# Layer kernel with a state-space scan on one Trainium2 core: both directions' scans in one instruction stream, more of the small work on VectorE, and a reordered step in the attention

## The chip, the cores and the metric

The kernel runs on one core of a Trainium2 chip. The core has TensorE (PE: matrix products, whose weights are loaded by a separate stream, PEld), VectorE (DVE), ScalarE (ACT), GpSimd (POOL) and SyncE (SP, which here only starts transfers). Each engine works through its own queue in order, and semaphores connect them. Transfers between DRAM and the on-chip memory go through queues that an engine's own instructions feed. The metric is device time of one execution in microseconds (us). TensorE's clock has two levels, 1.2 and 2.4 GHz, and the profile shows the granted one as a fraction of full speed.

## What is computed

Two layers act on 1024 latent and 256 context tokens of width 1024. In each layer a normalised, modulated input goes through one wide projection, whose output columns are shared among four mixers: an attention with 4 heads (A), a pooling mixer (B), a two-way complex state space (C) and a spatial gating (D). Their gated outputs go through one output projection and a normalisation. The change touches A, B and above all C:

```python
def _s5_scan(u, disc, reverse, h0):                       # 16 groups of 64 complex states
    lb_re, lb_im, bb_re, bb_im = disc
    bu_re = jnp.einsum('bngh,gph->nbgp', u, bb_re)        # and bu_im
    ...
    _, _, hr, hi = lax.associative_scan(_cscan_combine, (a_re, a_im, bu_re, bu_im),
                                        reverse=reverse, axis=0)   # h[t] = lb * h[t-1] + bu[t]

def _s5_readout(hr, hi, c_re, c_im):
    return jnp.einsum('nbgp,ghp->bngh', hr, c_re) - jnp.einsum('nbgp,ghp->bngh', hi, c_im)

def _pool_mixer(vin, w_pool, scale):                      # windows 2, 4, 8, 16
    ...                                                   # centred means minus the input
    y = jnp.einsum('bngc,gcd->bngd', pooled.reshape(b, n, N_POOL, POOL_GC), w_pool)
    return y.reshape(b, n, BRANCH_W) * scale

    # attention, for 128 queries at a time
    s = einsum('bqhd,bkhd->bhqk', qn, k_nope) + einsum('bqhr,bkr->bhqk', qr, k_rope)
    p = jax.nn.softmax(s * scale, axis=-1)
    return jnp.einsum('bhqk,bkhd->bqhd', p, vf)
```

In the second layer only the latent tokens' output is needed.

## The kernel before

All engines' instructions are written in program order in one file, and a scheduler places each engine's queue from it by that order as priority, except where the kernel fixes the order by hand (the attention, the first section and the output projection). Generators with `yield` are the unit in which `layer` (L1723 to L1928) interleaves the mixers' small work with the projection's weight blocks. A weight block is loaded (`wraw`), rounded on ScalarE into a high half (`whi`, L638), and VectorE takes the low half (`wlo`, helper line L131) as the difference. TensorE multiplies the high and low halves with the input's halves (L152 to L154), so a block's last third waits for VectorE. A generic helper at L131, L144 or L148 issues nearly all two-operand operations, so rows carry that line, and the tiles' names tell them apart.

The state space works on blocks of 8 tokens, 160 block positions ("slots": 128 latent, 32 context) in all.

- `s5_operators` (L505 to L634) makes a layer's operators. `outer` (L563 to L577) is six instructions on 128x512 elements: four products and two combinations. VectorE calls it for the input operators (tiles `op2`, `op3` and scratch `op0`). GpSimd calls it for the readout operators (tile `R`, one for all four calls, with the scratch `op1`), and GpSimd's queue then stores `R` to DRAM in two transfers (`Rd`). TensorE transposes the input operators (`tp_s5op`, L598), ScalarE copies and stores them (`Ed`). A short kernel of lags follows (`Kd`).
- `s5_states` (L733 to L758) loads the blocks' inputs, and TensorE makes what each slot adds to the state. ScalarE copies each PSUM tile to `H`, a tile [128, direction, 8, re/im, 161] with the slots in order along the last axis (L755 to L758). `H` lies on memory that the operators' pool (`ops`) has held.
- `s5_scan` (L760 to L854) cuts the 160 slots into 5 segments of 32 and advances all five at once, one slot per step, 31 steps. Each step and direction has a product of 160 elements (8 rows, two parts, two operands, 5 segments at a stride of 32) and two additions of 80, with the two directions interleaved. Ahead of it a table of powers (`pws`) is made, one direction on VectorE, the other on GpSimd. Behind it the segments are joined: for each of the four borders and each direction five small instructions carry the state, and five instructions on 496 or 248 elements fix up the segment. VectorE does five of these eight blocks, GpSimd three (`PFIX`). At the end four transfers on GpSimd's queue exchange the halves of `H` through DRAM (`Xd`, L850 to L853).
- `s5_readout` (L856 to L898) builds the short kernel's weights (`M`, ScalarE, L868) and makes the output on TensorE: for 16 operators each, one product with the inputs (L888), one with the backward states (L891), and with the forward states one (128 columns, L892) and in layer 0 another (32, L894). The moving operand is a contiguous stretch of `H`.
- `pool_mix` (L958 to L985) makes the windows' sums, on GpSimd for the first of its two blocks of channels (`b` 0) and on VectorE for the second.
- The attention's order is given by hand (L1480 to L1532): it passes over the queries, two heads at a time, and for each pass over pieces of the keys. In each pass, VectorE takes the rows' maxima (`maxima`), then at the mark `m4` the low parts of the next queries (`QA`, `QB`: two subtractions), then writes the maximum rows (`rows`, L144) that TensorE needs for the shift (L1376) and the sums (L1435).

## Time and profile before

| | us |
|---|---|
| median of 3 runs | 1434.23 (1432.74 to 1434.94) |
| profiled execution | 1430.7, span 1428.9 |
| TensorE busy, share of the span | 1252.1, 88% |
| VectorE busy | 932.5, 65% |
| GpSimd busy | 554.7, 39% |
| ScalarE busy | 467.6, 33% |
| mean granted clock of TensorE | 0.95 |

Busy times are of the profiled execution. Register, branch and transfer-starting instructions do not count as busy. In the timelines a line begins with its start and the time that the group on it spans, and ends with the idle time before it in brackets and what ended that, where that counts. `out<-in` are the tiles' names, `xN` how many instructions the line stands for.

### The profile page before, as it was taken

How to read it: one execution, taken by the hardware profiler on the slowest of the kernel's cores; microseconds unless marked ns; L12 is line 12 of the kernel's file. 1: busy time of each engine (PE TensorE's matmuls, PEld its weight loads, DVE VectorE, ACT ScalarE, POOL GpSimd, SP SyncE). 2: the span in 40 equal slices, each digit the busy share in tenths (PEclk: the TensorE clock that was granted, in tenths of full speed). 3: DMA queues.
4: the chain of work that ended last, by engine and by line, in shares of the span. 5: the costliest groups of instructions: out<-in, count | busy, mean ns of one | idle time of the engine just before them, and what ended most of it. 6: DMA issues, size and time to landing. Idle time of an engine off the chain costs nothing.

```text
span 1428.9 us, 19998 instructions
## 1 busy us (share of the span) xinstructions
PE 1252.1 (88%) x7556; PEld 962.6 (67%) x7556; DVE 932.5 (65%) x1812; ACT 467.6 (33%) x879; POOL 554.7 (39%) x580
## 2 busy tenths in 40 slices
PE   3877994999999998999999869987599998998997
PEld 1555773779878766666777647765488786665685
DVE  7685399642543566767798882599517456767666
ACT  2341130121244644445243322301213454544300
POOL 2467230500102254665444592224101136756443
PEclk9887997999999989999999979998889999999999
DMA  9435322476320100014123444412662020000421
GB/s 322 135 94 177 115 85 75 117 199 151 83 57 19 45 23 1 1 42 133 48 74 103 100 140 158 138 45 59 135 161 66 11 60 23 30 2 16 150 101 73
DMA packets 124677, 127.31 MB, mean 89 GB/s; under 512 B 40908, under 2 KB 98724, under 8 KB 124582
## 3 DMA queue, kind: packets, MB, share of 16 engines
q1 hardware_dynamic: 118886, 111.86, 26.8%
q0 software_dynamic: 2880, 9.54, 2.8%
q10 hardware_dynamic: 2816, 4.65, 0.9%
q8 instruction: 59, 0.97, 0.3%
q14 instruction: 36, 0.29, 0.1%
HBM read 97.47 MB, written 25.94 MB: 86 GB/s over the span
## 4 chain that ended last, share of the span: by engine, by line
PE 51%; DVE 29%; POOL 6%; issue 6%; DMA 4%; ACT 3%; SPq 1%; DVEq 0%; POOLq 0%; ACTq 0%
PE mm_out L1637 7%; PE mm_sc L1332 6%; PE mm_in L154 6%; PE mm_in L152 6%; PE mm_in L153 6%; DVE H L131 5%; DVE stmp L131 3%; DVE z L148 3%; DVE acc L131 2%; PE av L1415 2%; DVE op L131 2%; PE mm_sc L1374 1%; POOL op L131 1%; DMA M<-Kd 1%; DVE xres L145 1%
## 5 line engine op out<-in xcount | busy, mean ns | idle before, releaser
L154 PE MATMUL mm_in<-hT,wlo 128*128 128x512 f32 (+1 forms) x696 | 264.9, 381 | 26.0 <-DVE wlo L131 26.0
L153 PE MATMUL mm_in<-hT,whi 128*128 128x512 f32 (+1 forms) x696 | 265.1, 381 | 5.0 <-POOL hT L131 2.5
L152 PE MATMUL mm_in<-hT,whi 128*128 128x512 f32 (+1 forms) x696 | 269.0, 388 | 0.4 <-ACT whi L638 0.4
L154 PEld LDWEIGHTS mm_in<-hT,wlo 128*128 128x128 f32 x696 | 136.8, 197 | 53.6 <-DVE wlo L131 28.7
L1637 PE MATMUL mm_out<-wo,yh 128*128 128x512 f32 x576 | 164.2, 398 | 1.8 <-DVE wo L131 1.7
L152 PEld LDWEIGHTS mm_in<-hT,whi 128*128 128x128 f32 x696 | 136.6, 197 | 36.9 <-issue 14.2
L153 PEld LDWEIGHTS mm_in<-hT,whi 128*128 128x128 f32 x696 | 136.5, 196 | 31.4 <-POOL hT L131 5.3
L1637 PEld LDWEIGHTS mm_out<-wo,yh 128*128 128x128 f32 x576 | 107.3, 188 | 29.9 <-DVE wo L131 3.3
L638 ACT CAST whi<-wraw 128x1024 fp32r<-128x1024 f32 x38 | 42.6, 1121 | 194.6 <-PE mm_in L153 146.8
L131 DVE TENSOR_TENSOR wlo<-wraw,whi 128x1024 fp32r<-128x1024 f32 x38 | 58.0, 1530 | 68.0 <-ACT whi L638 61.7
L131 DVE TENSOR_TENSOR acc<-acc,mm_sc 128x512 f32<-128x512 f32 x108 | 74.2, 687 | 42.3 <-PE mm_sc L1332 31.2
L131 POOL TENSOR_TENSOR psum<-pE 128x512 f32<-128x512 f32 (+1 forms) x36 | 47.4, 1318 | 124.2 <-ACT pE L1393 124.1
L1637 PE MATMUL mm_out<-wo,yl 128*128 128x512 f32 x288 | 93.1, 395 | 0.3 <-POOL yl L131 0.3
L131 POOL TENSOR_TENSOR psum<-psum,pL 128x512 f32<-128x512 f32 x64 | 83.2, 1300 | 6.4 <-ACT pL L1393 1.5
L131 DVE TENSOR_TENSOR H<-H,stmp 128x80 f32<-128x80 f32 x248 | 74.6, 355 | 0.8
L144 POOL TENSOR_SCALAR rs_z<-mv_z 128x1 f32<-128x1 f32 x18 | 18.5, 1029 | 119.9 <-DVE mv_z L1669 119.9
L144 POOL TENSOR_SCALAR srs<-smv 128x1 f32<-128x1 f32 x18 | 5.6, 310 | 152.6 <-DVE smv L1065 152.6
L1637 PEld LDWEIGHTS mm_out<-wo,yl 128*128 128x128 f32 x288 | 54.2, 188 | 13.4 <-POOL yl L131 0.8
L131 DVE TENSOR_TENSOR stmp<-a,H 128x160 f32<-128x160 f32 x124 | 53.3, 462 | 14.6 <-POOL pws L131 7.2
L1393 ACT ACTIVATE pE<-mm_sc 128x512 f32<-128x512 f32 x55 | 30.7, 595 | 95.0 <-PE mm_sc L1374 73.7
L1621 ACT CAST yh<-G 128x1024 fp32r<-128x1024 f32 x18 | 18.9, 1052 | 115.1 <-PE mm_out L1637 113.8
L1788 ACT ACTIVATE G<-mm_in 128x512 f32<-128x512 f32 (+1 forms) x40 | 22.2, 555 | 104.1 <-PE mm_in L154 104.0
(361 smaller groups left out, 2789.8 us busy)
## 6 DMA issues: line engine op xcount, KB each, us to landing
wmod<-in_w_mod_dram SPq DMA_DIRECT2D x48, 512.0 KB, 4.3
wraw<-in_w_in_dram SPq DMA_DIRECT2D x36, 512.0 KB, 4.1
wor<-in_w_out_dram SPq DMA_DIRECT2D x16, 512.0 KB, 3.5
s5u<-Sd SPq DMA_DIRECT2D x8, 640.0 KB, 7.3
xd<-z SPq DMA_DIRECT2D x10, 512.0 KB, 2.7
xin<-in_x_dram SPq DMA_DIRECT2D x8, 512.0 KB, 7.6
Ed<-E ACTq DMA_DIRECT2D x16, 256.0 KB, 3.0
Rd<-bldR POOLq DMA_DIRECT2D x16, 256.0 KB, 3.9
```

What stands on the lines that cost most here:

```text
L131: return e.tensor_tensor(out=out, in0=a, in1=b, op=op)
L144: return e.tensor_scalar(out=out, in0=a, scalar1=s1, scalar2=None, op0=op0)
L148: return V.scalar_tensor_tensor(out=out, in0=a, scalar=s, in1=b, op0=op0, op1=op1)
L152: T.matmul(out, lhsT=ahi, rhs=bhi, start=start, stop=False)
L153: T.matmul(out, lhsT=ahi, rhs=blo, start=False, stop=False)
L154: T.matmul(out, lhsT=alo, rhs=bhi, start=False, stop=stop)
L638: copy(hi, raw)
L1332: T.matmul(out, lhsT=K[:, e, 128 * kt_:128 * kt_ + 128], rhs=Q[:, f], start=(x == 0 and y == 0), stop=False, skip_group_check=True)
L1393: S.activation(out=p, in_=ps, func=AF.Exp, scale=QSCALE)
L1415: T.matmul(st[v][64 * h:64 * h + 64, 0:n], lhsT=Vt[:, BANKS[i // 2][i % 2], 64 * head:64 * head + 64], rhs=st[v, h]["pt"][i // 2][:, n * ( ...
L1637: T.matmul(a[1][nh], lhsT=y[u][:, k, :], rhs=self.W[k][:, v, 512 * nh:512 * nh + 512], start=(k == 0 and u == 0 and v == 0), stop=(k == KC ...
L1788: S.activation(out=G[ci][:, b, :], in_=ps, func=AF.Silu)
```

## The change

Four things are done.

1. The operators of the readout go from GpSimd to VectorE (`outer(V, ...)`). They stand behind all state operators and lag kernels, share their scratch tile, and alternate between `R` and a new tile `R2`, which lies in the operators' pool. Their eight stores stay on GpSimd's queue.
2. `H` holds the slots with the segments innermost: the five segments' slots of one step lie side by side (165 positions instead of 161), and the backward direction is stored mirrored. ScalarE's copies into `H` write with a stride of 5 elements, and so the moving operands in `s5_readout` are read. A scan step is one product of 320 elements and two additions of 160 for both directions. The table is made on VectorE alone. The four carries come in a row for both directions, and the fix-ups are 16 instructions on 8 x 31 x 4 elements, all on VectorE.
3. `pool_mix` of the first block goes from GpSimd to VectorE.
4. In the attention the mark `m4` (the next queries' low parts) stands behind the maximum rows.

```diff
-NPOS = 161
+NPOS = 165
 SEG = 32
-PFIX = (1, 2, 3)
...
-        tv_, tp_, w0, w1, BC = (sp.tile([128, 1024], F32, name="op%d" % i) for i in range(5))
+        tv_, R2, w0, w1, BC = (sp.tile([128, 1024], F32, name="op%d" % i) for i in range(5))
...
-            first = mul(e, a, lr, vr)
-            if e is P:
-                tc.keep_in_program_order(first)
+            mul(e, a, lr, vr)
             mul(e, b, li, vi)
             tt(e, dre, a, b, ALU.subtract if sgn > 0 else ALU.add)
             mul(e, a, lr, vi)
...
-            Rv = R.rearrange("p (r c q) -> p r c q", r=2, c=4)
             for c in (slice(0, 4), slice(4, 8)):
                 k0, step = ((7, -1), (0, 1))[d]
                 outer(V, tv_, ld, k0, step, [Bb[:, ri, 8 * d:8 * d + 8, :] for ri in range(2)], c, [w[:, c] for w in W], 1)
-
-                k0, step = ((1, 1), (8, -1))[d]
-                outer(P, tp_, ld, k0, step, [CT[:, ri, 8 * d:8 * d + 8, :] for ri in range(2)], c,
-                      [Rv[:, ri] for ri in range(2)], -1)
-                for ri in range(2):
-                    P.dma_start(Rd[l][:, c, 2 * d + ri, :], Rv[:, ri])
                 yield
-            yield
...
         P.dma_start(Kd[l][112:128, :], dd)
+        for d in range(2):
+            for i, c in enumerate((slice(0, 4), slice(4, 8))):
+
+                k0, step = ((1, 1), (8, -1))[d]
+                Rv = (R, R2)[i].rearrange("p (r c q) -> p r c q", r=2, c=4)
+                outer(V, tv_, 2 * l + d, k0, step, [CT[:, ri, 8 * d:8 * d + 8, :] for ri in range(2)], c,
+                      [Rv[:, ri] for ri in range(2)], -1)
+                for ri in range(2):
+                    P.dma_start(Rd[l][:, c, 2 * d + ri, :], Rv[:, ri])
+                yield
         drop("ops")
...
+    NSEG = NSLOT // SEG
+
+    def spread(x, dims):
+
+        return bass.AP(tensor=x.tensor, offset=x.offset, ap=[list(x.ap[0])] + dims)
...
         Hs[0] = H
-        V.memset(H[:, 0, :, :, 0:1], 0.0)
-        V.memset(H[:, 1, :, :, NSLOT:NPOS], 0.0)
+        V.memset(H[:, :, :, :, 0:1], 0.0)
         for d in range(2):
             for ri in range(2):
                 E = wr("Eld")
...
                     pv = ps[:, 0:np_ * NSLOT].rearrange("p (j c) -> p j c", j=np_)
-                    hv = H[:, d, p0:p0 + np_, ri, :]
+
+                    pv = pv.rearrange("p j (a b) -> p j a b", b=SEG)
+                    h = [[2 * NPOS, np_]]
                     if d:
-                        S.copy(hv[:, :, 0:NSLOT], pv)
+                        S.copy(spread(H[:, d, p0, ri, NPOS - 1:NPOS], h + [[-1, NSEG], [-NSEG, SEG]]), pv)
                     else:
-                        S.copy(hv[:, :, 33:NPOS], pv[:, :, 0:128])
-                        S.copy(hv[:, :, 1:33], pv[:, :, 128:NSLOT])
+                        S.copy(spread(H[:, d, p0, ri, NSEG + 1:NSEG + 2], h + [[1, NSEG - 1], [NSEG, SEG]]), pv[:, :, 0:NSEG - 1])
+                        S.copy(spread(H[:, d, p0, ri, NSEG:NSEG + 1], h + [[NSEG, SEG]]), pv[:, :, NSEG - 1])
...
-
-        for d in range(2):
-            for c in range(2):
-                tc.keep_in_program_order(E[d].tensor_copy(T2[:, d, c, :, 0], a8[:, l, d, :, 0, c]))
+        T2 = tab.rearrange("p (c x i) -> p c x i", c=2, x=16)
+        a8l = a8[:, l].rearrange("p d r k o -> p (d r) k o")
...
+
+        def states_at(i, dims):
...
+        for c in range(2):
+            V.tensor_copy(T2[:, c, :, 0], a8l[:, :, 0, c])
...
         while n < SEG:
...
+            b = [T2[:, c, :, n - 1:n].to_broadcast([128, 16, n]) for c in range(2)]
+            x = [T2[:, c, :, 0:n] for c in range(2)]
+            o = [T2[:, c, :, n:2 * n] for c in range(2)]
...
+            mul(V, o[0], b[0], x[0])
+            mul(V, m1, b[1], x[1])
+            mul(V, o[1], b[0], x[1])
+            mul(V, m2, b[1], x[0])
+            sub(V, o[0], o[0], m1)
+            add(V, o[1], o[1], m2)
             n *= 2
...
-            o = 160 * (2 * d + i % 2)
-            return tmp[:, o:o + 32 * n].rearrange("p (r k o s) -> p r k o s", r=8, k=2, o=2)
-
         for i in range(1, SEG):
-            xs_ = []
-            for d in range(2):
-                st = (SEG, -SEG)[d]
-                h = H[:, d, 0, 0, position(d, i - 1):position(d, i - 1) + 1]
-                x = x_tile(i, d, nseg)
-                mul(V, x.rearrange("p r k o s -> p (r k) o s"),
-                    a8[:, l, d].rearrange("p r k o -> p (r k) o").unsqueeze(3).to_broadcast([128, 16, 2, nseg]),
-                    ap(h, [[NPOS, 16], [0, 2], [st, nseg]]))
-                xs_.append(x)
+            x = tmp[:, 320 * (i % 2):320 * (i % 2) + 64 * NSEG].rearrange("p (x k o s) -> p x k o s", x=16, k=2, o=2)
+            mul(V, x.rearrange("p x k o s -> p (x k) o s"),
+                a8l.rearrange("p x k o -> p (x k) o").unsqueeze(3).to_broadcast([128, 32, 2, NSEG]),
+                states_at(NSEG * i, [[NPOS, 32], [0, 2], [1, NSEG]]))
+            h = states_at(NSEG * i + NSEG, [[2 * NPOS, 16], [NPOS, 2], [1, NSEG]])
...
-                for d in range(2):
-                    h = H[:, d, 0, 0, position(d, i):position(d, i) + 1]
-                    h = ap(h, [[2 * NPOS, 8], [NPOS, 2], [(SEG, -SEG)[d], nseg]])
-                    add(V, h, h, xs_[d][:, :, k])
+                add(V, h, h, x[:, :, k])
             yield
...
+        xc = sml.tile([128, 64], F32, tag="xc", name="xc", bufs=1)
+        x1, x2 = (xc[:, 32 * i:32 * i + 32].rearrange("p (x o) -> p x o", x=16) for i in range(2))
+        re, im = (T2[:, c, :, SEG - 1:SEG].to_broadcast([128, 16, 2]) for c in range(2))
+        for k in range(1, NSEG):
+            h, hc = (states_at(NSEG * SEG + j, [[2 * NPOS, 16], [NPOS, 2]]) for j in (k - 1, k))
+            mul(V, x1, re, h)
+            mul(V, x2, im, h)
+            add(V, hc, hc, x1)
+            sub(V, hc[:, :, 0], hc[:, :, 0], x2[:, :, 1])
+            add(V, hc[:, :, 1], hc[:, :, 1], x2[:, :, 0])
+        V.tensor_copy(states_at(1, [[NPOS, 32], [1, NSEG - 1]]), states_at(NSEG * SEG, [[NPOS, 32], [1, NSEG - 1]]))
+        yield
...
-        mv_ = [s2("sm1")[:, 0:496], s2("sm2")[:, 0:496]]
-        mp_ = [tmp[:, 0:496], tmp[:, 496:992]]
...
-            for d in range(2):
-                e, (m1, m2) = (P, mp_) if (d == 1 and k in PFIX) else (V, mv_)
-                prev = position(d, SEG * k - 1)
-                re, im = (T2[:, d, c, :, 0:w].unsqueeze(2).to_broadcast([128, 8, 2, w]) for c in range(2))
-                h = H[:, d, :, :, prev:prev + 1].to_broadcast([128, 8, 2, w])
-                c0 = position(d, SEG * k)
-                cur = ap(H[:, d, 0, 0, c0:c0 + 1], [[2 * NPOS, 8], [NPOS, 2], [(1, -1)[d], w]])
-                mul(e, m1, re, h)
-                mul(e, m2, im, h)
-                add(e, cur, cur, m1)
-                c_re = ap(H[:, d, 0, 0, c0:c0 + 1], [[2 * NPOS, 8], [(1, -1)[d], w]])
-                c_im = ap(H[:, d, 0, 1, c0:c0 + 1], [[2 * NPOS, 8], [(1, -1)[d], w]])
-                sub(e, c_re, c_re, m2[:, :, 1])
-                add(e, c_im, c_im, m2[:, :, 0])
-            yield
+        m = tmp[:, 0:8 * w * (NSEG - 1)].rearrange("p (r i s) -> p r i s", r=8, i=w)
+        for d in range(2):
+            re, im = (T2[:, c, 8 * d:8 * d + 8, 0:w].unsqueeze(3).to_broadcast([128, 8, w, NSEG - 1]) for c in range(2))
+            for o in range(2):
+                own, other = (states_at((16 * d + y) * NPOS + 1, [[2 * NPOS, 8], [0, w], [1, NSEG - 1]]) for y in (o, 1 - o))
+                cur = states_at((16 * d + o) * NPOS + NSEG + 1, [[2 * NPOS, 8], [NSEG, w], [1, NSEG - 1]])
+                mul(V, m, re, own)
+                add(V, cur, cur, m)
+                mul(V, m, im, other)
+                tt(V, cur, cur, m, ALU.add if o else ALU.subtract)
+                yield
...
 
-                    T.matmul(o, lhsT=R_[:, 1, :], rhs=H[:, 1, pr, g, 1:1 + nr], start=False, stop=False)
-                    T.matmul(o[:, 0:128], lhsT=R_[:, 0, :], rhs=H[:, 0, pr, g, 32:160], start=False, stop=last)
+                    ov = o.rearrange("p (a b) -> p a b", b=SEG)
+                    T.matmul(ov, lhsT=R_[:, 1, :], rhs=spread(H[:, 1, pr, g, NSLOT - 1:NSLOT], [[-1, nr // SEG], [-NSEG, SEG]]),
+                             start=False, stop=False)
+                    T.matmul(ov[:, 0:NSEG - 1], lhsT=R_[:, 0, :], rhs=spread(H[:, 0, pr, g, 1:2], [[1, NSEG - 1], [NSEG, SEG]]),
+                             start=False, stop=last)
                     if not last:
-                        T.matmul(o[:, 128:160], lhsT=R_[:, 0, :], rhs=H[:, 0, pr, g, 0:32], start=False, stop=True)
+                        T.matmul(ov[:, NSEG - 1], lhsT=R_[:, 0, :], rhs=spread(H[:, 0, pr, g, 0:1], [[NSEG, SEG]]),
+                                 start=False, stop=True)
...
     def pool_mix(l, b, v, last):
         stg[0] = "pool"
-        e = V if b else P
+        e = V
         n = 1040 if last else 1312
...
                 k = [range(5 * h + i, 5 * h + j) for i, j in PVS]
                 vals(v, w, k, 0)
                 maxima(v, h)
-                go("m4")
                 vals(v, w, k, 1)
                 rows(v, h)
+                go("m4")
                 go("row")
                 vals(v, w, k, 2)
```

## Rows read from the trace of the kernel before

**Rows 1.** Windows of four stretches: length, busy us of PE, PEld, DVE, ACT, POOL, clock, DMA

```profile
85.80:172.00 86.20, 69.14 (x421) 54.90 (x421) 50.69 (x74) 20.88 (x45) 51.63 (x73) 0.86 0.44 138
172.00:276.00 104.00, 84.88 (x514) 64.15 (x510) 92.60 (x267) 17.70 (x36) 31.99 (x38) 0.90 0.29 88
797.00:870.00 73.00, 53.79 (x272) 44.43 (x271) 55.31 (x57) 22.49 (x51) 56.72 (x49) 0.86 0.44 124
903.00:1047.00 144.00, 112.02 (x553) 82.06 (x552) 108.20 (x296) 27.33 (x60) 41.01 (x72) 0.89 0.39 100
```

**Rows 2.** Timeline of TensorE, the largest waits: start, duration, group, idle before

```profile
135.38 1.08 PE L598 MATMUL tp_s5op<-ident,op 128*128 128x128 f32 x4 [9.01 <-DVE op L131]
243.38 1.22 PE L994 MATMUL tp_pool<-pv,wpool 128*128 128x256 f32 x2 [12.15 <-DVE G L148]
852.30 0.58 PE L154 MATMUL mm_in<-hT,wlo 128*128 128x256 f32 x1 [10.33 <-DVE wlo L131]
977.80 1.08 PE L245 MATMUL mm_mod<-wmod,sT 128*32 128x256 f32 x8 [8.00 <-DMA wmod<-in_w_mod_dram]
1035.41 0.69 PE L1018 MATMUL tp_sgup<-sgw 128*64 128x128 f32 x2 [12.52 <-ACT sgw L1010]
```

**Rows 3.** Groups of VectorE, 79 to 139 us (busy, mean ns, idle); VectorE's timeline, layer 1

```profile
L131 DVE TENSOR_TENSOR op<-lamT,op 128x512 f32<-128x512 f32 x16 | 20.3, 1295 | 0.2
...
886.05 1.29 DVE L131 TENSOR_TENSOR op<-lamT,op 128x512 f32<-128x512 f32 x2
887.44 0.69 DVE L131 TENSOR_TENSOR op<-op 128x512 f32<-128x512 f32 x1
```

**Rows 4.** Timeline of VectorE in layer 0's scan

```profile
199.47 5.18 DVE L131 TENSOR_TENSOR H<-H,stmp 128x80 f32<-128x80 f32 x4
```

**Rows 5.** The page's list of transfers: instructions, size, median from issue to landing

```profile
Rd<-bldR POOLq DMA_DIRECT2D x16, 256.0 KB, 3.9
```

**Rows 6.** Timeline of VectorE, scan steps of layer 0

```profile
184.45 0.44 DVE L131 TENSOR_TENSOR stmp<-a,H 128x160 f32<-128x160 f32 x1
184.93 0.64 DVE L131 TENSOR_TENSOR H<-H,stmp 128x80 f32<-128x80 f32 x2
185.60 0.45 DVE L131 TENSOR_TENSOR stmp<-a,H 128x160 f32<-128x160 f32 x1
...
191.02 0.81 DVE L131 TENSOR_TENSOR stmp<-a,H 128x160 f32<-128x160 f32 x2
...
192.57 0.82 DVE L131 TENSOR_TENSOR stmp<-a,H 128x160 f32<-128x160 f32 x2
```

**Rows 7.** Groups of VectorE, pooled sums of layer 1

```profile
L131 DVE TENSOR_TENSOR p<-pw 128x1039 f32<-128x1039 f32 x1 | 1.2, 1235 | 0.0
```

**Rows 8.** Timeline of GpSimd at the end of layer 1's scan

```profile
1007.67 1.69 POOL L851 DMA_DIRECT2D Xd<-H  x2 [6.35 <-DVE H L131]
1021.12 0.84 POOL L853 DMA_DIRECT2D H<-Xd  x1 [11.76 <-DMA Xd<-H]
```

**Rows 9.** ScalarE, tiles `H` and `M`: ns min/median/max, first and last start, forms

```profile
L755 ACT COPY H<-tp_s5st x12: 428/561/566, 181.8 to 917.0; 128x480 f32<-128x480 f32 x8, 128x320 f32<-128x320 f32 x4
L868 ACT COPY M<-M x32: 421/454/495, 312.4 to 1033.1; 128x128 f32<-128x128 f32 x32
```

**Rows 10.** Timeline of TensorE in layer 0's readout

```profile
324.75 0.44 PE L891 MATMUL tp_s5rd<-H,Rld 128*128 128x160 f32 x2
325.03 0.38 PE L892 MATMUL tp_s5rd<-H,Rld 128*128 128x128 f32 x2
```

**Rows 11.** Timeline of VectorE in layer 0's attention

```profile
581.49 0.42 DVE L1356 TENSOR_REDUCE mx<-tp_mx 128x2 f32<-128x256 f32 x1 [0.62 <-PE tp_mx L1354]
...
583.18 0.48 DVE L144 TENSOR_SCALAR row<-tp_mx,par 128x256 fp32r<-128x256 f32 x1
...
592.84 0.48 DVE L144 TENSOR_SCALAR row<-tp_mx,par 128x256 fp32r<-128x256 f32 x1 [0.53 <-PE tp_mx L1363]
```

**Rows 12.** Waits of TensorE in layer 0's attention: us in total, times, longest

```profile
PE tp_sm L1435 <- DVE row L148: 4.4, 6, 1.5
```

35 lines of the change are left out of this document (2 added, 33 removed).

## Prediction

> **What bounds the kernel now.** I first read the windows by stage, then TensorE's waits, then who held them up. [rows 1] are four stretches: the state-space operators of layer 0, its scan, and the same two of layer 1. Each shows TensorE's busy time beside the length and the granted clock. TensorE is idle 17.1, 19.1, 19.2 and 32.0 us in them, 87 us together; outside them it is nearly full. Its clock has two levels, so a mean of 0.86, 0.90, 0.86 and 0.89 says that 24, 21, 20 and 32 us ran at 1.2 GHz, partly inside the idle time, partly on matmuls just behind it. [rows 2] are the largest waits: on VectorE's operators (9.0), on a product queued behind the scan (12.2), on the low half of a weight (10.3), on a load whose buffer such a low half holds (8.0), and in the tail of layer 1's scan (12.5). So these stretches are bound by VectorE's in-order queue. Why it is late is in [rows 3]: a 128x512 product of the operators takes 1295 ns on average in layer 0 while GpSimd works on the readout operators, and 1.29 us for two, one every 0.65, with GpSimd idle. [rows 4] is the same in the scan: four additions take 5.18 us beside the pooled sums, against about 0.9.
>
> **Readout operators on VectorE.** 24 instructions per layer leave GpSimd. On VectorE three take 2.08 us ([rows 3]: from 886.05 to the end of the row at 887.44) and a gap of some 0.04 to the next, so 24 take 17.0. They share the scratch tile with the state operators and follow them in program order, so they start after the last of these. In layer 0 I put that near 116, and TensorE's matmuls into the state near 153 (172 now), so 17 us and the store of the last tile, about 4 us of flight [rows 5] plus its issue, are covered. In layer 1 the room is small: H lies on the memory of the operator pool, and the new tile R2 belongs to that pool, so H's first eviction waits until R2's store has landed. Queued behind it are ScalarE's other evictions, TensorE's state products (two PSUM tiles) and then the scan. I count 3 us there; with the cover gone it is 17 + 5 = 22, the bound. The eight stores per layer stay on GpSimd's queue, now with no arithmetic ahead of them; the two alternating tiles give each store 8.5 us before its tile is written again, so I price that at nothing, and at one flight, 4 us, per reuse if not.
>
> What this takes away in layer 0: state operators at 0.65 instead of 1.3 us finish before TensorE asks, so most of the 17.1 us of idle time and the slow matmuls behind go. The clock's share lies between (24 - 17)/2 = 3.5 and 12 us. **I take 18** of at most 29, because weight loads and the normalised inputs still end some waits. In layer 1, 797 to 870, the wait of 10.3 goes and about 2 us of slow matmuls; the rest hangs on the output projection's tail, which is not touched. **I take 12** (8 to 16).
>
> **The scan's steps.** Now a direction alone needs 1.15 us per step, three instructions each waiting for the one before ([rows 6], 184.45 to 185.60: 0.44 and 0.64 busy, 0.07 between), and both interleaved 1.55 (191.02 to 192.57). The new step is one chain: a product of 320 elements and two additions of 160, five adjacent elements at a time. Contiguous rows give 0.69 for 512 [rows 3] and 1.235 for 1039 [rows 7], 1.03 ns per element, so 0.49 and 0.33; with three waits of 0.03 a step is 1.25. 31 steps: 38.8 instead of 48, -9. If adjacent fives cost like today's stride (0.44 for 160, 0.7 ns per element more), it is 1.7 us and +5. I take 1.25, nearest to the contiguous rows, as five neighbours are closer to these. The scan cannot start before both directions are in H; now the first runs ahead, which costs about 6 us of start that the old scan used at 1.15 per step.
>
> **Fix-ups, carries, table, pooled sums.** Fix-ups: 16 instructions of 992 elements, 1.2 us each by [rows 7], 19 us; before, VectorE had five of eight blocks, 25 instructions of 496 or 248 elements, 10.2 us at 1.03 ns and about 12 with their starts; GpSimd had three, beside which VectorE was slowed. The carries become 20 small instructions instead of 40, -2. The power table is built in one go on VectorE, about 1.5 us more there, and GpSimd's part, which ended late in layer 1, goes. Pooled sums of the first block: four long instructions of 1.2 to 1.5 us and small ones, 6.8 us in layer 0 and 5.4 in layer 1. For these three (+7, +1.5, +6.8) GpSimd's arithmetic goes from the scan's stretch and with it the contention: adding up what VectorE's instructions there took above the same shapes elsewhere, with [rows 4] as the largest single piece, I get about 18 us per layer. VectorE's 92.6 us in the stretch of layer 0 [rows 1] so become 92.6 - 9 + 7 - 2 + 1.5 + 6.8 - 18 = 79, an estimate.
>
> **What that is worth.** In layer 0 the readout follows much later, so only TensorE's waits count: 19.1 idle plus at most 10 of clock. With one dependent chain, ready weight halves can be placed between its links; I leave 5 us of wait and 2 for slower evictions. **I take 16** (4 to 26). In layer 1 the scan's end counts itself: H goes out to DRAM and comes back ([rows 8]: store at 1007.67, return issued at 1021.12 after 11.76 of waiting; I put the landing at 1031, an estimate), and the first readout products came near 1047, behind the weight block that stalled with the rest. The new scan starts about 4 to 6 us later by its own clock, ends near 998 and is back near 1022, with that block already done: 1047 - 1022 = 25, less 7 for a cold clock after the remaining wait and the state phase. **I take 18** (3 to 28).
>
> **Strided evictions and readout.** H now has the segments innermost, so a contiguous run of slots lies 5 elements apart. ScalarE writes 480 contiguous elements in 0.56 us and 128 at a stride of 8 in 0.45 [rows 9]; the contiguous line through 320 (0.43) and 480 gives 0.27 for 128, so 1.4 ns per element extra: 5120 elements per layer, up to 7 us on ScalarE, of which two PSUM tiles let through 2 (counted above). TensorE: two passes of 160 columns took 0.28 us [rows 10] (324.75 to 325.03), 0.88 ns per column. 16 products per layer read H: 2 x 16 x 320 = 10240 columns in layer 0 and 2 x 16 x 256 = 8192 in layer 1. No row shows TensorE with a strided moving operand. Below nothing is excluded, as the same columns are read. Bounds: 0, and ScalarE's 1.4 ns on all 18432, +26. I take VectorE's strided read, 1.75 ns per element against 0.88, since it is also a read: **+16**, all of it on the path.
>
> The Trainium skill (SBUF — State Buffer, "Door 1: The DMA port swizzle", the box on cachelines) says that SBUF has 16-byte lines and full bandwidth needs at least two hits per line. It speaks for the scan's adjacent fives and against evictions and readout, where every element is on a new line. ScalarE's rows agree; the page prices nothing, so the sum would be as above with the rule on TensorE and 16 us less without.
>
> **Attention.** The two subtractions for the queries' low parts sit between the maximum and the rows. In passes without them the row starts 0.53 us after the maximum, when TensorE's transposes arrive; with them 583.18 - 581.91 = 1.27 [rows 11]. So the row comes 0.74 earlier in 9 + 7 = 16 passes, 11.8 us at most. TensorE waits for it at the sums' matmul 4.4 us in 6 waits in layer 0 [rows 12], at the shift similarly. The subtractions then precede the reciprocal, which waits for the sums anyway, and the queries are needed a pass later. **I take 7** (3 to 10).
>
> **Sum.** 18 + 16 + 12 + 18 + 7 - 16 = 55. From the profiled 1430.7 (span 1428.9 and 1.8 around it) that is 1375.7; the median of the runs stands 3.5 above the profiled one, so **1379**.
>
> **Rivals.** *Waits stay on VectorE* (0.20): weight halves remain queued behind a chain as long as before, so the two scan stretches give 4 and 8. For it: the queue is in order, and low halves held TensorE 10.3 and 8.0 us [rows 2]. Against: a chain of dependent links leaves slots. Sum 33, 1401. *TensorE reads strided H at no price* (0.13): columns take 0.88 ns already, twice the pace of the projections; 16 us less, 1363. *VectorE becomes a worse bound* (0.09): the fix-ups, 19 us plus 3 of carries, are flushed in one piece before a weight half that TensorE needs; I take half of it as covered by projections already loaded, so some 11 us of new wait and 4 of clock per layer, and neither scan stretch gains: -18 - 12 - 7 + 16 + 30 = +9, 1443. It decides once the new wait passes about 10 us per layer. *The operators do not get out of the way* (0.04): H is held by R2 the full 22 us in each layer, 1379 + 44 = 1423. My forecast keeps 0.54 (1360 to 1396).
>
> **How the numbers follow.** The range takes in the forecast, the first rival with its spread and the second: 1348 to 1414, about 0.83 of the chance. 0.2% (3 us) is about what a measurement of this kernel can tell from no change. Faster 0.88; same 0.03, the edges of the last two; slower 0.09.
>
> **What would show it.** Layer 0's operators: VectorE's 128x512 near 0.68 us throughout, the wait of 9.0 gone. Scan: a product of 320 near 0.49, a step near 1.25, low halves less than 3 us behind their high halves. Layer 1: H's first eviction not much behind the last state products, readout near 1022 minus the shifts before. Readout: two passes of 160 columns in 0.28 (free) or 0.56. Attention: row 0.53 behind the maximum in every pass. It is wrong if the step is near 1.7, if strided columns cost over 3 ns, or if TensorE's idle time in the four stretches stays above 60 us.

## The result and the profile after

| | before | changed |
|---|---|---|
| median, us | 1434.59 (1432.74 to 1436.2, 4 runs) | 1387.27 (1386.44 to 1391.8, 4 runs) |
| profiled execution, us | 1430.7 | 1387.97 (span 1386.2) |
| TensorE busy, us | 1252.1 | 1270.6 (92%) |
| VectorE busy, us | 932.5 | 899.5 (65%) |
| GpSimd busy, us | 554.7 | 412.9 (30%) |

The ratio of the times is 0.9681 (95% interval 0.9656 to 0.9706): 47.3 us less, of 55 forecast. The same four stretches as in [rows 1] stand below for the changed kernel, those of layer 1 moved by the 20.7 us by which that layer starts earlier; the columns are those of [rows 1].

```profile
85.80:172.00 86.20, 79.57 (x566) 61.90 (x566) 50.95 (x99) 30.78 (x60) 11.83 (x20) 0.96 0.52 170
172.00:276.00 104.00, 101.75 (x554) 76.33 (x552) 84.57 (x177) 17.82 (x30) 3.63 (x10) 0.98 0.49 128
776.30:849.30 73.00, 64.94 (x366) 52.65 (x365) 41.82 (x62) 27.01 (x58) 17.77 (x17) 0.93 0.46 132
882.30:1026.30 144.00, 138.31 (x738) 109.70 (x739) 91.42 (x189) 33.47 (x61) 6.76 (x20) 0.96 0.49 118
```

TensorE's idle time in them is 6.6, 2.3, 8.1 and 5.7 us, 23 in place of 87, and the granted clock rose from 0.86 to 0.90 to 0.93 to 0.98. None of the five waits of [rows 2] is left at its size. So far the forecast holds. Where the time went by stage is read from the first matmul of each stage in TensorE's timeline, for the two profiled executions (1430.7 and 1387.97, 42.7 us apart):

| from, to | before, us | changed, us | difference |
|---|---|---|---|
| start to first matmul of layer 0's attention inputs | 463.7 | 436.8 | -26.9 |
| layer 0's attention to the first output projection | 184.5 | 190.7 | +6.2 |
| output projection 0 | 129.5 | 129.6 | 0 |
| layer 1's first projection to its attention inputs | 351.1 | 323.0 | -28.1 |
| layer 1's attention to its output projection | 154.7 | 161.1 | +6.4 |
| output projection 1 | 99.4 | 99.3 | 0 |

The attention inputs themselves, which lie between these rows, change by 0.5 us at most. The state-space stages gave 55 us, more than the 48 that their terms (18 + 16 + 12 + 18 - 16) promised (1.2 of the 55 had come before the operators' first matmul, at 84.3 and 83.0 us), and the attentions lost 12.6, where the forecast had them gain 7. The two attentions as windows, before and after (columns as in [rows 1]):

```profile
479.40:663.90 184.50, 166.97 (x1157) 117.61 (x1155) 120.29 (x200) 89.86 (x177) 107.06 (x94) 0.95 0.07 21
1165.50:1320.20 154.70, 140.59 (x1036) 100.62 (x1034) 106.26 (x174) 77.23 (x150) 93.65 (x80) 1.00 0.06 20
```

```profile
452.50:643.20 190.70, 173.06 (x1156) 123.09 (x1154) 125.13 (x200) 89.95 (x177) 106.22 (x94) 0.92 0.06 20
1116.20:1277.30 161.10, 146.46 (x1037) 104.80 (x1035) 109.13 (x174) 77.25 (x150) 92.85 (x80) 0.96 0.06 19
```

The same matmuls are busy 6 us longer in each, idle time stays (17.5 and 17.6 in layer 0, 14.1 and 14.6 in layer 1), and the clock falls from 0.95 to 0.92 and from 1.00 to 0.96. So it isn't more waiting but slower matmuls. TensorE's waits in layer 0's attention say what changed ahead of them (us in total, times, longest):

```profile
PE tp_mx L1338 <- DVE acc L130: 7.1, 6, 2.1
PE mm_sc L1358 <- DVE row L147: 2.2, 2, 1.1
PE tp_sm L1419 <- DVE row L147: 2.1, 6, 1.2
```

The wait of [rows 12] fell from 4.4 to 2.1 as forecast, the shift's beside it from 4.1 to 2.2. What the rows gained came back at the next transposes of the maxima, which wait for VectorE's running maximum `acc`: 3.1 us before, at most 1.0 at once, now 7.1, with three stalls of 2.1. Layer 1 has three of 2.1 as well; before, its longest was 1.7. The matmuls behind such a stall are slow. TensorE's row that ends the first one in layer 0, and two windows behind it (columns as in [rows 1]; the clock is 0.53 and then 1.00):

```profile
547.08 0.62 PE L1338 MATMUL tp_mx<-ident,acc 128*128 128x128 f32 x2 [2.11 <-DVE acc L130]
```

```profile
547.00:549.00 2.00, 1.92 (x8) 0.83 (x8) 0.42 (x1) 0.00 (x0) 1.88 (x3) 0.53 0.00 0
551.00:553.00 2.00, 2.00 (x17) 1.64 (x18) 0.85 (x2) 1.50 (x3) 0.34 (x1) 1.00 0.01 4
```

### The profile page after: what moved, and what is told of

Read it like the earlier page. It is cut to its first block, busy times and chain, and to the rows that moved or that the text cites. A ratio compares the mean times of both kernels' runs of the same rounds, so it can differ in the third digit from the quotient of the medians.

```text
span 1386.2 us, 19652 instructions
## 1 busy us (share of the span) xinstructions
PE 1270.6 (92%) x7556; PEld 977.2 (70%) x7556; DVE 899.5 (65%) x1636; ACT 475.8 (34%) x879; POOL 412.9 (30%) x418
## 4 chain that ended last, share of the span: by engine, by line
PE 54%; DVE 28%; issue 6%; ACT 5%; POOL 4%; DMA 3%; SPq 1%; DVEq 0%; POOLq 0%; ACTq 0%
PE mm_out L1621 7%; PE mm_in L151 6%; PE mm_in L152 6%; PE mm_in L153 6%; PE mm_sc L1316 6%; PE av L1399 4%; DVE acc L130 3%; DVE H L130 3%; DVE z L147 3%; DVE stmp L130 2%; DVE op L130 2%; DVE xres L144 1%; PE mm_sc L1358 1%; DVE wlo L130 1%; PE tp_sc L1316 1%
## 5 line engine op out<-in xcount | busy, mean ns | idle before, releaser
L153 PE MATMUL mm_in<-hT,wlo 128*128 128x512 f32 (+1 forms) x696 | 261.2, 376 | 0.0
L151 PEld LDWEIGHTS mm_in<-hT,whi 128*128 128x128 f32 x696 | 133.9, 193 | 35.2 <-issue 12.2
L152 PEld LDWEIGHTS mm_in<-hT,whi 128*128 128x128 f32 x696 | 134.1, 193 | 31.5 <-POOL hT L130 6.4
L153 PEld LDWEIGHTS mm_in<-hT,wlo 128*128 128x128 f32 x696 | 133.9, 193 | 24.5 <-issue 1.6
L130 DVE TENSOR_TENSOR wlo<-wraw,whi 128x1024 fp32r<-128x1024 f32 x38 | 48.5, 1276 | 37.8 <-ACT whi L637 37.8
L130 DVE TENSOR_TENSOR H<-H,stmp 128x160 f32<-128x160 f32 (+1 forms) x140 | 59.4, 424 | 4.1
L1316 PE MATMUL mm_sc<-QA,KT 96*128 96x256 f32 x372 | 57.2, 311 | 0.0
L1316 PEld LDWEIGHTS mm_sc<-QA,KT 96*128 96x128 f32 x372 | 52.6, 214 | 6.4 <-issue 6.3
```

Source lines behind the costliest of these rows:

```text
L130: return e.tensor_tensor(out=out, in0=a, in1=b, op=op)
L151: T.matmul(out, lhsT=ahi, rhs=bhi, start=start, stop=False)
L152: T.matmul(out, lhsT=ahi, rhs=blo, start=False, stop=False)
L153: T.matmul(out, lhsT=alo, rhs=bhi, start=False, stop=stop)
L1316: T.matmul(out, lhsT=K[:, e, 128 * kt_:128 * kt_ + 128], rhs=Q[:, f], start=(x == 0 and y == 0), stop=False, skip_group_check=True)
```

## The experiments

Each run was compared with the kernel before on the same chip, whose median was 1434.6 us beside the change, 1435.1 beside e1 to e4, 1437.1 beside e5, e6, e8 and e10, and 1434.7 beside e7 and e11 to e13. So two runs are compared better by their ratios than by their medians; where the two disagree, both are given. The last two columns are from one trace each: from the start to layer 0's attention inputs, and from layer 1's first projection to its own. They differ by up to 4 us between runs whose edits lie elsewhere (the change, e1 and e10).

| run | median, us | ratio to before (95%) | layer 0 | layer 1 |
|---|---|---|---|---|
| the change | 1387.3 | 0.9681 (0.9656 to 0.9706) | 436.8 | 323.0 |
| e1_m4_back | 1375.7 | 0.9602 (0.9555 to 0.9649) | 433.2 | 319.4 |
| e2_m4_alone | 1443.9 | 1.0061 (1.0023 to 1.0099) | 462.5 | 352.1 |
| e3_flat_readout | 1367.7 | 0.9549 (0.9488 to 0.9610) | 429.4 | 315.4 |
| e4_ops_gpsimd | 1419.0 | 0.9897 (0.9863 to 0.9930) | 456.6 | 332.1 |
| e5_pool_gpsimd | 1399.0 | 0.9733 (0.9692 to 0.9775) | 446.3 | 327.7 |
| e6_old_scan | 1412.3 | 0.9826 (0.9777 to 0.9876) | 445.8 | 342.5 |
| e7_scan_alone | 1429.8 | 0.9953 (0.9933 to 0.9973) | 465.3 | 344.7 |
| e8_adjacent_readout | 1361.1 | 0.9475 (0.9436 to 0.9513) | 427.9 | 313.4 |
| e10_dve_early | 1367.6 | 0.9527 (0.9489 to 0.9564) | 436.3 | 320.4 |
| e11_all_adjacent | 1349.8 | 0.9391 (0.9360 to 0.9421) | 428.2 | 311.6 |
| e12_early_adjacent | 1354.2 | 0.9429 (0.9400 to 0.9458) | 428.1 | 314.5 |
| e13_r2_first | 1379.8 | 0.9624 (0.9578 to 0.9669) | 437.0 | 320.0 |

### The fourth part: undone, and alone

```diff
                 maxima(v, h)
+                go("m4")
                 vals(v, w, k, 1)
                 rows(v, h)
-                go("m4")
```

> The changed kernel with the fourth part undone: the queries' low parts stand ahead of the maximum rows again. Theory A (the moved subtractions cost time): between the start of the attention's matmuls and the start of the output projection the changed kernel took 6.2 us (layer 0) and 6.4 us (layer 1) more than before, all of it in stretches at the lower clock that follow stalls of 2.1 us on the transposes of the maxima. Undone, these 12.6 us come back: 1387.3 - 12.6 = 1374.7 us, the stalls of 2.1 us are near 1.0, and the time at the lower clock in the two attentions falls from 44 us to about 17. Rival B (the attention is slower for another reason, the state it inherits from the new stages, and the move itself gives what was forecast): 1387.3 + 7 = 1394. Rival C (the lower clock falls where chance has it): within 4 us of 1387.

Measured 1375.7, 11.6 less: theory A. The attentions take 184.5 and 156.5 us, and no stall of 2.1 is left:

```profile
448.90:633.40 184.50, 167.01 (x1157) 117.65 (x1155) 120.52 (x200) 89.84 (x177) 107.07 (x94) 0.95 0.07 21
1102.70:1259.20 156.50, 142.20 (x1036) 102.13 (x1034) 107.54 (x174) 77.28 (x150) 93.58 (x80) 0.99 0.06 20
```

The reverse edit in the kernel before:

> The kernel before with the fourth part alone. Theory A: the two attentions take 12.6 us longer, 1434.6 + 12.6 = 1447. Rival B: 1434.6 - 7 = 1427.6. Rival C: within 4 us of 1434.6. Everything outside the attentions is expected to stay, in all three.

Measured 1443.9; by the ratio 9 us more (the interval allows 3 to 14): theory A in sign, somewhat less in size. Its ten runs lie between 1434 and 1456, and the profiled one, the fastest, is the instructive one: layer 1's attention has the three stalls of 2.1 us in it, but its clock is 1.00 and it takes 155.0 us, 0.3 more than before. There the stalls themselves cost next to nothing, since the waits for the rows shrink as they grow. What costs is the lower clock that follows such a stall: in the traces of the change and of e2 to e4 it follows 12 of 24. Shorter stalls are followed by it too, one of 1.5 us in layer 0's attention before among them, so the stalls' length alone does not decide it, and what does is not shown.

### Why VectorE is late: the early subtraction

VectorE's timeline in one pass of the changed kernel, from the maximum on, with GpSimd's first addition of that pass below it (a second view; the tile `psum` holds row sums and lies in SBUF, not in PSUM):

```profile
536.78 0.42 DVE L1340 TENSOR_REDUCE mx<-tp_mx 128x2 f32<-128x256 f32 x1 [0.78 <-PE tp_mx L1338]
...
538.65 0.41 DVE L130 TENSOR_TENSOR QA<-qp,QA 64x256 fp32r<-64x256 f32 x1
539.09 0.42 DVE L130 TENSOR_TENSOR QB<-qp,QB 64x256 fp32r<-64x256 f32 x1
539.58 1.76 DVE L1423 RECIPROCAL rs<-tp_sm 128x256 f32<-128x256 f32 x1
541.37 1.43 DVE L130 TENSOR_TENSOR qr<-qf,qr 128x256 fp32r<-128x256 f32 x1
...
545.80 1.13 DVE L130 TENSOR_TENSOR acc<-acc 128x256 f32<-128x256 f32 x1
```

```profile
541.22 1.29 POOL L130 TENSOR_TENSOR psum<-pE 128x512 f32<-128x512 f32 x1 [4.64 <-ACT pE L1377]
```

The subtraction of `qr` starts 0.15 us behind GpSimd's addition and ends 0.29 behind its end (541.22 + 1.29 = 542.51). The same pass before, VectorE and then GpSimd:

```profile
562.92 0.42 DVE L1356 TENSOR_REDUCE mx<-tp_mx 128x2 f32<-128x256 f32 x1 [0.95 <-PE tp_mx L1354]
...
566.00 1.76 DVE L1439 RECIPROCAL rs<-tp_sm 128x256 f32<-128x256 f32 x1 [0.84 <-PE tp_sm L1435]
567.68 0.36 DVE L131 TENSOR_TENSOR qr<-qf,qr 128x256 fp32r<-128x256 f32 x1
...
571.42 0.77 DVE L131 TENSOR_TENSOR acc<-acc 128x256 f32<-128x256 f32 x1
```

```profile
567.64 1.55 POOL L131 TENSOR_TENSOR psum<-pE 128x512 f32<-128x512 f32 x1 [5.08 <-ACT pE L1393]
```

There it took 0.36, and it was GpSimd's addition that took 1.55. All seven passes in which this subtraction stands behind a reciprocal are alike: 0.36 us before, 1.12 to 1.45 in the changed kernel. Counted from the maximum, the reciprocal starts 0.28 us earlier now (2.80 behind it, not 3.08), and a wait of 0.28 for a score is gone; the subtraction takes 1.07 and the last maximum 0.36 more. Net 0.87 late, about the 1.1 that the stall grew. GpSimd's addition, too, comes 0.28 earlier, so it starts 1.64 us behind the reciprocal in both kernels; what moved against it is the subtraction, by 0.11 (0.15 behind it now, 0.04 before). If the collision is what makes VectorE late, the subtraction only has to go ahead of the reciprocal:

```diff
                 rows(v, h)
                 go("m4")
+                go("dve")
                 go("row")
 ...
                     go("fdve")
-                go("dve")
```

> The changed kernel, with the low part of the rotated queries (a subtraction of 128x256) taken right behind the subtractions of the fourth part, ahead of the reciprocal, where GpSimd still rests. Theory A (the stalls of 2.1 us come from GpSimd's first addition, which starts just before that subtraction and holds it for 1.43 in place of 0.36 us): the subtraction takes 0.4, the stalls on the maxima's transposes fall to about 1.3 us, and with them some of the lower clock: 1378 to 1384 us. Rival B (VectorE's queue is full in any order, and the reciprocal starts later by what the subtraction gains): stalls of 2 us stay, 1387 within 4.

Measured 1367.6, 19.7 less than the changed kernel (22 by the ratios): theory A, though its range of 1378 to 1384 had the gain too small. VectorE's pass, and the two attentions:

```profile
538.79 0.42 DVE L130 TENSOR_TENSOR qr<-qf,qr 128x256 fp32r<-128x256 f32 x1
539.14 1.75 DVE L1423 RECIPROCAL rs<-tp_sm 128x256 f32<-128x256 f32 x1
...
544.27 0.54 DVE L130 TENSOR_TENSOR acc<-acc 128x256 f32<-128x256 f32 x1
```

```profile
452.10:634.10 182.00, 168.67 (x1157) 120.39 (x1155) 119.53 (x200) 89.91 (x177) 106.10 (x94) 0.94 0.07 22
1104.90:1257.60 152.70, 142.08 (x1036) 102.13 (x1034) 104.99 (x174) 77.19 (x150) 92.76 (x80) 0.99 0.06 20
```

The subtraction takes 0.42, the waits for `acc` in layer 0 fall from 7.1 to 1.7 us, and the attentions take 182.0 and 152.7 us. Against before that is 4.5 us less, inside the 3 to 10 that the forecast gave the part, but with two steps moved and not one. What the early subtraction gives without the fourth part was not run.

The Trainium skill (SBUF — State Buffer, "SBUF: two separate sides") says that VectorE, when it reads two operands from SBUF, and GpSimd hold a shared port by turns, and whichever starts first keeps it for its whole instruction. These rows agree that one of the two is held: the subtraction in the changed kernel (1.43 for 0.36), the addition before (1.55 for 1.29), while VectorE's additions that read PSUM keep their 0.67 to 0.69 throughout. Who starts first they cannot tell: before, the subtraction is recorded 0.03 to 0.06 us behind the addition in six of the seven passes, and yet it is the addition that is held; in the changed kernel it is recorded 0.13 to 0.45 behind. Whether that tenth of a microsecond is the cause of the hold or part of it stays open.

### The readout's columns

```diff
-rhs=spread(H[:, 1, pr, g, NSLOT - 1:NSLOT], [[-1, nr // SEG], [-NSEG, SEG]])
+rhs=spread(H[:, 1, pr, g, 1:2], [[SEG, nr // SEG], [1, SEG]])
...                                   # the same for the forward direction
```

> The changed kernel, whose readout reads the same number of columns of H in memory order and not every fifth, so that its output takes the states of other slots; all else stays. TensorE's busy time in the readout was 36.8 and 26.5 us before and 46.4 and 34.9 after. Theory A (the strided columns cost 0.8 ns each more, and all of it lies on the path): the busy time returns to about 37 and 26.5 and the run is 1387.3 - 18 = 1369. Rival B (other waits fill the place, since TensorE also works on other blocks there and the readout waits for its weights): half or less of that comes back, 1378 or more.

Measured 1367.7, with 36.7 and 26.7 us for the readout: theory A. These figures, and the "busy time" of the expectations, add up the products' durations, which overlap; counted once, TensorE is busy with them 24.9 and 19.6 us in the changed kernel and 16.6 and 12.4 here, 15.5 less. From the first state product to the attention inputs layer 0 takes 7.4 us less, and layer 1 from its start 7.6, so nearly all of the 15.5 lies on the path. Over all traces the first of these stages takes 280.0 to 282.5 us with the columns at a stride (the change, e1, e10, e13) and 273.5 to 275.8 without (e3, e8, e11, e12), the second 319.4 to 323.0 and 311.6 to 315.4, so 13 to 15 us for both layers together. Then the same states in memory order, the result at a stride instead:

```diff
-ov = o.rearrange("p (a b) -> p a b", b=SEG)
+ov = o.rearrange("p (a b) -> p b a", b=SEG)
-rhs=spread(H[:, 1, pr, g, NSLOT - 1:NSLOT], [[-1, nr // SEG], [-NSEG, SEG]])
+rhs=spread(H[:, 1, pr, g, NSLOT - 1:NSLOT], [[-NSEG, SEG], [-1, nr // SEG]])
...                                   # the same for the forward direction
```

> The version with the fourth part undone (1375.7), and the readout's products walk the columns in the order in which they lie in memory, four or five adjacent ones at a time, while the result is written to PSUM at a stride of 32. Theory A (what costs is that each read column lies apart from the last): TensorE's busy time in the readout falls from 46.5 and 35.0 to 38 and 28 or less, and the run takes 1375.7 - 15 = 1361. Rival B (any pattern of the moving operand that is not one run costs the full price, or the strided result costs as much): no change, 1372 to 1380. Rival C (the strided result costs more than it saves): above 1380.

Measured 1361.1, 14.6 less than e1_m4_back by the medians and 18 by the ratios; the durations add up to 37.1 and 26.7 us: theory A. That the median met 1361 to the microsecond is luck, since the two traces differ by 10.2 us in the state-space stages from the first state product on. Two passes of 160 columns, in the changed kernel and then in this one:

```profile
288.04 0.72 PE L872 MATMUL tp_s5rd<-H,Rld 128*128 128x160 f32 x2
288.58 0.64 PE L874 MATMUL tp_s5rd<-H,Rld 128*128 128x128 f32 x2
```

```profile
285.93 0.43 PE L872 MATMUL tp_s5rd<-H,Rld 128*128 128x160 f32 x2
286.20 0.38 PE L874 MATMUL tp_s5rd<-H,Rld 128*128 128x128 f32 x2
```

From one start to the next 0.54 us became 0.27: 1.69 and 0.84 ns per column, with [rows 10] at 0.88.

### The operators, the pooled sums and the scan

The first part undone puts `outer(P, ...)` and its stores back between the state operators, as in the kernel before.

> The changed kernel with the first part undone: the readout operators on GpSimd between the state operators. Theory A (what I forecast, 18 + 12 us for this part): VectorE's products of 512 in the operators of layer 0 are near 1.3 us again, TensorE waits some 9 us for them, and the run takes 1387.3 + 30 = 1417. Rival B (the gain came from the scan, which would have followed the operators' lateness anyway): under 10 us more, 1397 or less. Rival C (with the scan's other work gone from GpSimd it may even be better off with them, because VectorE gets 17 us per layer back): 1380.

Measured 1419.0, 31.7 more: theory A, and by layer as well (19.8 us in layer 0, where 18 was taken, 9.1 in layer 1, where 12 was). VectorE's products are at 1.27 us again, its low halves at 2.4, and TensorE waits for them (groups of VectorE in layer 0's operators, then a row of TensorE's timeline):

```profile
L130 DVE TENSOR_TENSOR op<-lamT,op 128x512 f32<-128x512 f32 x16 | 19.9, 1270 | 0.1
...
L130 DVE TENSOR_TENSOR wlo<-wraw,whi 128x1024 fp32r<-128x1024 f32 x3 | 7.2, 2404 | 0.0
```

```profile
138.47 1.09 PE L597 MATMUL tp_s5op<-ident,op 128*128 128x128 f32 x4 [13.40 <-DVE op L130]
```

The third part undone:

```diff
     def pool_mix(l, b, v, last):
-        e = V
+        e = V if b else P
```

> The changed kernel with the third part undone: the first block's pooled sums on GpSimd. They then lie beside the scan. Theory A (contention on single instructions of VectorE, as in the 5.18 us of the kernel before, about as much as the 6.8 and 5.4 us that the sums take on VectorE): in layer 0 TensorE hardly notices, in layer 1 the scan's end moves by under 4 us: within 5 us of 1387. Rival B (each addition of GpSimd holds a dependent link of the scan's chain, and weight halves queue behind it): 10 us or more slower, 1397 or above.

Measured 1399.0, 11.8 more by the medians, but 7.5 by the ratios, whose intervals overlap; so the rows must decide, and they speak for rival B. I had taken VectorE's own sums as an even trade for the contention. They aren't: the two additions of one scan step take 6.05 us, not 0.69, and TensorE's product behind them waits 9.65, not 0.5 (VectorE's and TensorE's timelines). In layer 1 the product behind the pooled sums waits 8.1, not 1.0:

```profile
192.47 6.05 DVE L130 TENSOR_TENSOR H<-H,stmp 128x160 f32<-128x160 f32 x2
```

```profile
216.34 1.22 PE L978 MATMUL tp_pool<-pv,wpool 128*128 128x256 f32 x2 [9.65 <-DVE G L147]
```

The second part undone (the states, the scan and the readout of the kernel before, with its 161 positions):

> The changed kernel with the second part undone: slots in their old order, both directions' chains of their own, GpSimd with its share of table and fix-ups, and the readout's columns contiguous again. Theory A (my terms: the scan was worth 16 + 18, the strided columns cost 16 to 18): 1387.3 + 34 - 17 = 1404. Rival B (the operators' move gave most, and the new scan only pays for its own strided columns): within 4 us of 1387. Rival C (with the operators out of the way GpSimd's share beside the scan does no harm, and the old scan's readout is cheaper): 1375. In all of them TensorE's busy time in the readout is near 36.8 and 26.5 us.

Measured 1412.3, 25.0 more by the medians and 21 by the ratios: nearest to theory A, 4 to 8 beyond it. TensorE has two long waits in layer 1's scan again, on a low half and on `sgw`, as in [rows 2]:

```profile
982.92 0.79 PE L154 MATMUL mm_in<-hT,wlo 128*128 128x512 f32 x1 [13.56 <-DVE wlo L131]
...
1012.08 0.69 PE L1018 MATMUL tp_sgup<-sgw 128*64 128x128 f32 x2 [13.09 <-ACT sgw L1010]
```

And the second part alone in the kernel before:

> The kernel before with the second part alone. Theory A (the parts add; undoing the scan cost 25 us in the changed kernel): 1434.6 - 25 = 1410. Rival B (the scan's gain needs the other parts: with the operators late and the pooled sums on GpSimd beside it, TensorE's waits stay, and the strided readout takes its 18 us): 1430 or more.

Measured 1429.8, 5 to 7 less: rival B. In layer 0 nothing is gained (465.3 us to the attention inputs, 463.7 before), since the operators are late as ever, and the pooled sums on GpSimd lie beside the new chain. TensorE's wait for the operators:

```profile
138.36 1.09 PE L598 MATMUL tp_s5op<-ident,op 128*128 128x128 f32 x4 [12.52 <-DVE op L131]
```

So the scan is worth 21 to 25 us with the other parts and 5 to 7 without. Undone one at a time, the parts cost 31.7, 25.0, 11.8 and -11.6 by the medians, 57 together for a change worth 47; by the ratios it is 48 for 46. How much of the gain needs several parts at once is thus not settled by these sums; that some of it does is shown by the second part alone.

### H's hold in layer 1

```diff
-                Rv = (R, R2)[i].rearrange("p (r c q) -> p r c q", r=2, c=4)
+                Rv = (R2, R)[i].rearrange("p (r c q) -> p r c q", r=2, c=4)
```

> The changed kernel with the two tiles of the readout operators exchanged, so that the last store reads the tile outside the operators' pool, and H is free when VectorE has done its last combination, about 3.5 us before it is now (879.8 in layer 1, where the last store of the pool's tile lands). Theory A (in layer 1 TensorE has enough other blocks meanwhile, so H's hold costs little): H's first copy about 3.5 us earlier, the run within 3 us of 1387. Rival B (the scan's end decides in layer 1, so what the scan's start gains is gained): 1387.3 - 3.5 = 1384, hardly to be told apart by the time alone; the start of the readout in layer 1 against the start of the layer tells it: 221.4 us in the changed kernel, 218 by B.

Measured 1379.8; the intervals of the two ratios overlap, so the time decides nothing. The rows do. Changed kernel first (GpSimd's last store from the pool's tile, ScalarE's first copy to `H`, VectorE's first scan step), then this one:

```profile
876.88 0.75 POOL L631 DMA_DIRECT2D Rd<-op  x1 [1.58 <-DVE pws L130]
880.26 0.88 ACT L762 COPY H<-tp_s5st 128x384 f32<-128x384 f32 x1
893.02 0.49 DVE L130 TENSOR_TENSOR stmp<-a,H 128x320 f32<-128x320 f32 x1 [11.51 <-ACT H L760]
```

```profile
872.87 0.75 POOL L631 DMA_DIRECT2D Rd<-op  x1 [2.82 <-DVE pws L779]
878.04 0.87 ACT L762 COPY H<-tp_s5st 128x384 f32<-128x384 f32 x1 [5.61 <-DVE bldR L130]
890.82 0.49 DVE L130 TENSOR_TENSOR stmp<-a,H 128x320 f32<-128x320 f32 x1 [4.54 <-ACT H L760]
```

Against the layer's first projection (773.4 and 775.2) the first copy comes 4.0 us earlier, the scan's first step 4.0 and the readout 4.2 (217.2, not 221.4; e1, e3, e8, e10 and e12, with the old order, lie between 220.4 and 221.2). Rival B as far as the readout: in layer 1 the scan's start decides when it starts. The attention inputs come 3.0 earlier, but in e1, where nothing here was changed, 3.6; so what reaches the end is not shown.

### The best version

The early subtraction with the readout in memory order, and then ScalarE's copies into `H` in memory order as well:

```diff
-pv = pv.rearrange("p j (a b) -> p j a b", b=SEG)
+pv = pv.rearrange("p j (a b) -> p j b a", b=SEG)
-S.copy(spread(H[:, d, p0, ri, NPOS - 1:NPOS], h + [[-1, NSEG], [-NSEG, SEG]]), pv)
+S.copy(spread(H[:, d, p0, ri, NPOS - 1:NPOS], h + [[-NSEG, SEG], [-1, NSEG]]), pv)
...                                   # the same for the forward direction
```

> As the run before, with ScalarE's copies left as in the changed kernel. Theory A (early subtraction and adjacent readout columns lie in different stages and add): 1367.6 - 14.6 = 1353. Rival B (the clock in the attention gives part of it back, as it falls anew in each kernel): 1357 to 1362.

> The version with the early subtraction of the rotated queries (1367.6), the readout's products in memory order (14.6 us in the version with the fourth part undone), and ScalarE's copies into H in memory order too, reading PSUM at a stride of 32. Theory A (all three gains add, and a copy of 480 falls from 1.0 to about 0.6 us): the scans start 3 us earlier in layer 1, nothing in layer 0 follows: 1367.6 - 14.6 - 3 = 1350. Rival B (the copies' order doesn't matter, since PSUM at a stride costs ScalarE what H at a stride costs): copies stay near 1.0 us and the time is that of the version without them, 1353.

Measured 1354.2 and 1349.8, where 1353 and 1350 were expected: the gains add. The last step can't be told from none by the times, whose intervals overlap, but by the rows: ScalarE's copy, changed kernel and last version (ns min/median/max):

```profile
L760 ACT COPY H<-tp_s5st x12: 725/998/1032, 165.1 to 892.3; 128x480 f32<-128x480 f32 x8, 128x320 f32<-128x320 f32 x4
```

```profile
L760 ACT COPY H<-tp_s5st x12: 417/560/563, 164.5 to 872.8; 128x480 f32<-128x480 f32 x8, 128x320 f32<-128x320 f32 x4
```

and the readout of layer 1 comes 217.4 us behind the layer's start, not 220.4. The last version takes 0.939 of the time before, 37 us less than the change as made.

## Why the prediction was right, and where it was wrong

**What bounds.** Right. VectorE's queue ahead of TensorE in four stretches was the bound, and 65 of the 87 us of idle time went.

**Readout operators.** The two terms of 30 together measured 31.7 when undone, 29 by the stages. The state products of layer 0 start at 154.3, where I put 153. The first step that was off is small: a combination into `R` or `R2`, which writes its result at a stride of 8 elements, takes 1.15 us and not 0.69, so the 24 instructions take 20.7 instead of 17 (+8 x 0.46). VectorE's timeline:

```profile
115.03 1.15 DVE L130 TENSOR_TENSOR bldR<-op 128x512 f32<-128x512 f32 x1
```

The second is the price of the hold in layer 1: I counted 3 us of delay; the store of `R2` alone holds the first copy to `H` 4 us, and the readout as much. As the operators themselves came earlier, `H` was still free sooner than before.

**Scan.** Each price of the new scan held:

```profile
171.06 0.49 DVE L130 TENSOR_TENSOR stmp<-a,H 128x320 f32<-128x320 f32 x1 [14.46 <-ACT H L760]
171.59 0.69 DVE L130 TENSOR_TENSOR H<-H,stmp 128x160 f32<-128x160 f32 x2
172.31 0.49 DVE L130 TENSOR_TENSOR stmp<-a,H 128x320 f32<-128x320 f32 x1
```

A step is 172.31 - 171.06 = 1.25 us, a fix-up instruction 1.19, 19 us in all. (VectorE's share of the old fix-ups was 14 us by its rows, 15 instructions of 0.66 and 10 of 0.41, and not about 12, so the +7 was +5. Its busy time in layer 0's window came to 84.6, not 79.) The term for what this gives TensorE was rather too low than too high: undone, the scan costs 21 to 25 us although it has 13 to 15 of strided columns in it, so 34 to 40 against 34. By the stages of e6_old_scan, with the strided columns added, layer 0 gives about 16, as forecast, and layer 1 about 27, not 18: its readout starts 22.5 us earlier, near the 25 that I had, and the 7 that I took off for a slow clock do not show. The first rival (waits stay on VectorE) is not this kernel but e7_scan_alone, where GpSimd keeps the operators and the pooled sums.

**Pooled sums.** I priced them inside VectorE's sum and never by themselves; alone they are 8 to 12 us, where theory A of e5_pool_gpsimd had less than 5. By its rows, what a GpSimd instruction costs here is less VectorE's excess over its own time than what waits behind the link that it holds.

**Strided readout.** Right: 1.69 ns per column against the 1.75 taken, 15.5 us busy and 13 to 15 on the path against 16. ScalarE's price was 0.9 ns per element, not 1.4. The Trainium skill (SBUF — State Buffer, "Door 1: The DMA port swizzle", the box on cachelines) was thus right to count against reads of every fifth element, and the readout in fives confirms it from the other side; but its sentence that any pattern in PSUM that isn't contiguous slows matmuls is not borne out by these fp32 products, where a result at a stride of 32 cost nothing (0.84 ns per column), and the measurement decides.

**Attention.** This is the term that failed: +7 forecast, -12.6 in the stages, -11.6 when undone. The steps up to the rows were right (0.53 behind the maximum where the clock is full, the wait for it 4.4 down to 2.1). The step that failed is "the subtractions then precede the reciprocal, which waits for the sums anyway": it put what comes behind the reciprocal at nothing. The reciprocal even starts 0.28 us earlier, but the next subtraction is then held by GpSimd's addition (1.43 in place of 0.36) where before it held that addition, the last maximum is 0.36 longer, and the stalls of 2.1 us that follow are in 12 of 24 cases followed by the lower clock. I looked at who waits for the moved step and not at what the later steps collide with. The 19.6 us that this missed were partly paid by the state space, which gave 7 more than forecast. In the profiled runs that leaves 42.7 of 55; the medians say 47.3, since the profiled run of before lies 3.9 below its median. That the total came within 8 of the forecast is thus in part luck: two errors of opposite sign.

## What to carry to other kernels

Where two engines get into each other's way on single instructions, small shifts can decide who pays: here a tenth of a microsecond between two recorded starts went with a microsecond more on VectorE, so an edit in a tight order is checked by the neighbours' starts, not only by the step that it moves. A layout that suits one consumer need not cost the others: walk the indices in the order of the memory that minds, and put the stride on the side that doesn't. Parts that lift the same wait can be worth little alone and much together, so try a part both undone and alone before it is called useless.

## What the runs showed of the hardware

- A moving operand read at every fifth 4-byte element took 1.69 ns per column, four or five adjacent elements at a time 0.84, against 0.88 contiguous in the kernel before. A result or a source in PSUM at a stride of 32 elements cost neither TensorE nor ScalarE (0.56 us for 480) anything.
- A 128x256 subtraction on VectorE with both operands in SBUF took 0.36 us or 1.43 beside the same GpSimd addition, which then took 1.55 or 1.29; between the two cases its recorded start moved by 0.11 us against the addition's.
- A stall of 2.1 us was followed by the lower clock in 12 of 24 cases, and in one attention in none of three (granted clock 1.00). The ten runs of e2_m4_alone lay between 1434 and 1456 us, at mean clocks of 0.931 to 0.948.
